# Row sums by GpSimd's queue, a fourth raw weight buffer, and later row sums for the last head, in a hybrid decoder trunk

## The chip, the cores and the metric

The kernel runs on one core of a Trainium2 chip. The metric is the device time of one execution in microseconds (us). The engines are named as the profile names them: PE (TensorE, the matmuls), PEld (its weight loads), DVE (VectorE), ACT (ScalarE), POOL (GpSimd) and SP (SyncE, which here only issues DMAs; SPq in the views).

## The reference

Two layers (DEPTH = 2) of one mixer sub-layer each, over 512 tokens (SEQ) and 16 meta tokens put ahead of them, with model width 1024, all in float32. A layer projects the normed input with one combined matrix, and mixes it in two ways at once: by causal pooling over windows of 2, 4, 8 and 16 tokens, and by latent attention with 8 heads (64 plain and 32 rotary dimensions for queries and keys, 64 for values). Both results are gated and projected back:

```python
# per layer, h = RMSNorm(x)
[u_pool | z_pool | c_q | c_kv | k_rope | z_mla | g_pool | g_mla] = h @ W_in
y_pool = W_pool_up( PoolMix(u_pool) * silu(z_pool) )
y_mla  = W_mla_up( MLA(c_q, c_kv, k_rope) * silu(z_mla) )
x = x + W_out( sigmoid(g_pool) * y_pool + sigmoid(g_mla) * y_mla )
# inside MLA, for each head, causal, over 16 + 512 positions
p = softmax(s)                 # divides by the row sum of exp(s)
o = p @ v
```

The output are the 512 tokens after both layers.

## The kernel before, in words

*Products.* Tokens stand on the free axis, 264 columns at a time (two halves of 528) in layer 0 and where meta tokens are needed, 512 at a time where they are not. Each float32 product is made of three matmuls of split operands (`mm3`, lines 211 to 213): a weight chunk is split into `whi` (ACT, L206) and `wlo` (DVE, L207), an activation into a high and a low part, `hh` and `hl` for the normed input.

*Weights.* `stream()` goes through a plan of weight products in chunks of 128 x 512 elements. `wload` gives a chunk a raw buffer (tag `raw`, 3 of them, filled by a 256 KB DMA on SP's queue, L136), and then splits it; `whi` and `wlo` have three buffers each. It is called four chunks ahead. A raw buffer is free again when the subtraction L207 has read it. The names behind `raw<-` are the matrices: `win`, then `wmu` (the attention's up projection) and so on.

*Order.* The program is recorded in one pass: `step()` records the next piece of the weight stream and adds its length to a clock (`clk`, in nanoseconds of matmul time); `after(ns, fn)` records `fn` when that clock is `ns` further on; `fill(...)` and `gap()` let the stream run between the steps of a head. `behind(ins, other)` makes an instruction wait for another one, here always the matmul that was newest when it was recorded (`newest[0]`), so that a DMA or copy isn't put far ahead of its place. `follow(ins, other)` sets an order only. Each engine, and each issuer of DMAs, then works through its instructions in order.

*A head.* `head(h, ...)` makes four blocks of scores (tile `S`), takes the causal mask and the maximum (L843), the exponential on ACT (L850, with row sums `rs`), and turns the probabilities into 32 x 32 blocks (`turn`; the 16 meta columns go by POOL into `pm`, L853). The blocks go through memory: `pdr<-attD` (L916) writes them, and `back()` reads them in four DMAs, `attE<-pdr` (L924), `BACK` = 7800 ns of matmul time later. ACT and DVE split attE into `th` and a rest (L972, L973), and `pv` multiplies it by the values (L994, L997). That product isn't yet divided by the row sums. DVE takes their reciprocals (L910), in a tile of 128 x 4. `back()` writes them to memory as one row (`rdr<-rs`, L927), `sums()` reads the row back as a broadcast onto 64 partitions (`cq<-rdr`, L934), two heads into one tile, and for each pair `gate()` multiplies the broadcast into the gate `silu(z_mla)` (POOL, L938, `u<-u,cq`). In `part2` the pair's product is multiplied by it (L1013), `LAG` = 2000 being the unit of its delay. All the writes and reads of this paragraph are on SP's queue, between the weight loads. A read of the broadcast waits on SP until the write has landed.

*Copies.* `prep(h)` puts together the keys and queries of a coming head, with copies on POOL: L817 and L819 for the keys (`kh`, `kl`), L821 for the queries (`qhl`). `ev_mu` evicts the up projection's accumulator (`mm`, one of four buffers) and stands near the end of the attention, with the eviction of `gm` (DVE L1058, ACT L1059) ahead of it.

Of the kernel before, what the change touches and what calls it, by code (L numbers as in the profile page):

```python
# [9 lines left out]
F32 = mybir.dt.float32  # L10
# [8 lines left out]
P = 128  # L19
# [8 lines left out]
H = 8  # L28
# [27 lines left out]
LAG = 2000.0  # L56
TAIL = (9000.0, 9000.0)
SPL = 240
BACK = 7800.0
LATE = 13000.0  # L60
# [21 lines left out]
def trunk(ctx, tc, xT, xrow, mrow, pos, win, wkr, wqb, wkb, wvb, wgr, wpu, wmu, wout, gains, const, yT):  # L82
    nc = tc.nc
    pe, act, dve, gp, sp = nc.tensor, nc.scalar, nc.vector, nc.gpsimd, nc.sync
# [3 lines left out]
    wp = ctx.enter_context(tc.tile_pool(name="wp", bufs=2))  # L88
# [7 lines left out]
    def nm(s):  # L96
        uid[0] += 1
        return f"{s}_{uid[0]}"

    def slot(tag, dt=F32, bufs=1, w=W):  # L100
        return sl.tile([P, w], dt, tag=tag, name=nm(tag), bufs=bufs)
# [4 lines left out]
    def att(tag):  # L106
        return sl.tile([P, NB * P], F32 if tag == "D" else F32R, tag=f"att{tag}", name=nm(f"att{tag}"), bufs=1 if tag == "D" else 2)
# [29 lines left out]
        return raw  # L137

    def rawt():
        return wp.tile([P, 512], F32, tag="raw", name=nm("raw"), bufs=3)  # L140

    early.append(slot("rinv"))
    act.dma_start(early[0][:, 0:512], win[0, MT_CKV, :, 0:512])
    first = sp.dma_start(gn, gains)
    sp.dma_start(xb[:, 0, :T], xT[:, 0, :])
    early.append(fetch(win[0, MT_CKV + 1, :, 0:512], 512, rawt(), sp))
    sp.dma_start(xb[:, 1, :T], xT[:, 1, :])
    xt = [xb[:, k] for k in range(8)]
# [16 lines left out]
    def other_loads(made):  # L165
        for k in range(2, 8):
            behind(sp.dma_start(xb[:, k, :T], xT[:, k, :]), made)
            if k in (3, 4):
                raw = rawt()
                behind(sp.dma_start(raw, win[0, MT_CKV + k - 3, :, 512:1024]), made)  # L170
                early.append(raw)
        behind(sp.dma_start(cst, const), made)
        behind(sp.dma_start(posb[:, :T], pos.partition_broadcast(P)), made)
        dve.tensor_copy(maskw[:, 512 - P:], cst[:, C_MASK:C_MASK + P])
# [18 lines left out]
    def wload(src, n, spare, home=None):  # L193
        if home is not None:
            raw = home
            behind(sp.dma_start(raw, src), marks[-4])
        else:
            raw = early.pop(0) if early else fetch(src, n, rawt(), sp)
        loads[0] += 1
        marks.append(newest[0])  # L200
        if loads[0] <= 2 or spare:
            t = wide()
            hi, lo = t[:, 0:512], t[:, 512:1024]
        else:
            hi, lo = (wp.tile([P, 512], F32R, tag=t, name=nm(t), bufs=3) for t in ("whi", "wlo"))
        act.activation(hi[:, :n], raw[:, :n], AF.Copy)  # L206
        dve.tensor_sub(lo[:, :n], raw[:, :n], hi[:, :n].bitcast(F32))  # L207
        return hi, lo
# [7 lines left out]
    newest = [None]  # L216
# [64 lines left out]
    def after(ns, fn):  # L281
        pend.append((clk[0] + ns, fn))
        pend.sort(key=lambda e: e[0])
# [28 lines left out]
    def follow(ins, other):  # L312
        tc.add_manual_dep(ins.ins, other.ins.name,
                          mybir.DependencyInfo(mybir.DependencyClass.NoSync, mybir.DependencyReason.SCHED_ONLY))

    def behind(ins, other):
        tc.add_manual_dep(ins.ins, other.ins.name,
                          mybir.DependencyInfo(mybir.DependencyClass.Sync, mybir.DependencyReason.DATA))
# [35 lines left out]
    class Layer:  # L354
# [470 lines left out]
        def head(self, h, kq, prev):  # L825
            kh, kl, qh, ql = kq
            odd = h % 2
# [3 lines left out]
            rs = sm.tile([P, 5], F32, tag="rs", name=nm("rs"), bufs=2)  # L831
# [80 lines left out]
            row = rdr[self.l][h]  # L912
# [8 lines left out]
            def back():  # L921
                got.append(att("E"))
                for b in range(4):
                    read = sp.dma_start(got[0][32 * b:32 * b + 32, :].bitcast(F32).rearrange("k (a x) -> k a x", a=4),  # L924
                                        via[:, n * b:n * b + n].rearrange("(a k) x -> k a x", a=4))
                    behind(read, newest[0])
                follow(sp.dma_start(row.rearrange("a (p i) -> p (a i)", i=4), rs[:, 0:4]), read)  # L927
                after(BACK / 3, sums)

            def sums():  # L930
                if odd == 0:
                    self.rb = slot("cq11")
                rb = self.rb
                behind(sp.dma_start(rb[64 * odd:64 * odd + 64, 0:512], row.partition_broadcast(64)), newest[0])  # L934

            def gate():
                z, rb = self.zms[h // 2][:, NM:T].rearrange("p (i q) -> p i q", i=4), self.rb
                behind(gp.tensor_mul(z, z, rb[:, 0:512].rearrange("p (q i) -> p i q", i=4)), newest[0])  # L938

            after(BACK if h + 1 < H else BACK / 3, back)  # L940
            if odd == 1:
                after(LATE if h + 1 < H else BACK, gate)
            return h, got

        def meta_turn(self, pm):
# [362 lines left out]
```

## Time and profile before

| | |
|---|---|
| time, median of 3 runs | 755.31 us (753.53 to 755.49) |
| the profiled execution | 755.48 us |
| its span | 753.7 us |
| PE busy | 748.1 us, 99% |
| DVE, ACT, POOL busy | 562.3, 395.2, 241.8 us |
| granted TensorE clock | 1.000 |
| moved by DMA | 106.55 MB, 141 GB/s in the mean |

The time is that of the whole execution, 1.78 us more than the span, which goes from the first to the last instruction of the profile. A row of the timeline reads: start, duration, engine, line, operation, out<-in with the shapes; in brackets the idle time of the engine before it, and what ended it. A row of a list of waits reads: the engine and line that waited, what it waited for, the total in us, how often, and the longest. A tile's view gives the durations of its DMA issues in ns (min, median, max), and the first and last start.

### The profile page before, as it was taken

The numbers are of one execution on the slowest core, as the hardware profiler recorded it, in microseconds if no ns is written. First come the engines' busy times: TensorE is split into PE (matmuls) and PEld (weight loads), VectorE is DVE, ScalarE is ACT, GpSimd is POOL, SyncE is SP. The second block draws the span as 40 slices with busy tenths as digits, with TensorE's granted clock in tenths as the row PEclk, the third lists the DMA queues.
The fourth block names the chain that finished last, engine by engine and source line by source line (L and its number), as shares of the span: only waits on it lengthen the run. The fifth ranks groups of instructions, "written<-read, shape, count | busy, mean of one in ns | idle before, by whom it ended". The sixth has DMA issues, their size and how long they took to land.

```text
span 753.7 us, 14317 instructions
## 1 busy us (share of the span) xinstructions
PE 748.1 (99%) x5010; PEld 681.9 (90%) x5010; DVE 562.3 (75%) x1214; ACT 395.2 (52%) x864; POOL 241.8 (32%) x294
## 2 busy tenths in 40 slices
PE   9999999999999999999999999999999999999998
PEld 9999899999999999999997898887788888887887
DVE  5588777658999987694367478678589999966942
ACT  6755656554656555543254456455445665554321
POOL 2126404704552520161130264038043526102400
PEclk9999999999999999999999999999999999999999
DMA  8633223434766576425643332233356666763462
GB/s 280 179 103 118 70 81 91 112 96 142 206 163 177 170 202 176 129 91 165 183 135 91 108 113 73 82 91 107 105 151 216 181 175 189 203 167 98 129 223 87
DMA packets 72798, 106.55 MB, mean 141 GB/s; under 512 B 14051, under 2 KB 34915, under 8 KB 72726
## 3 DMA queue, kind: packets, MB, share of 16 engines
q1 hardware_dynamic: 72582, 105.38, 47.8%
q8 instruction: 39, 0.64, 0.4%
q14 instruction: 33, 0.27, 0.1%
q10 hardware_dynamic: 144, 0.26, 0.1%
HBM read 89.76 MB, written 15.85 MB: 140 GB/s over the span
## 4 chain that ended last, share of the span: by engine, by line
PE 94%; DMA 4%; SPq 1%; DVE 1%; ACT 0%; issue 0%; ACTq 0%; DVEq 0%
PE mm L211 28%; PE mm L213 28%; PE mm L212 28%; PE S L211 2%; PE S L213 2%; PE S L212 2%; DMA raw<-wmu 1%; PE o L994 1%; DMA rdr<-rs 1%; PE o L997 1%; PE S L891 1%; PE S L538 1%; PE S L504 0%; DMA raw<-win 0%; DMA cq<-rdr 0%; DMA xb<-xT 0%
## 5 line engine op out<-in xcount | busy, mean ns | idle before, releaser
L213 PE MATMUL mm<-hh,wlo 128*128 128x264 f32 (+2 forms) x1072 | 337.0, 316 | 0.0
L212 PE MATMUL mm<-hl,whi 128*128 128x264 f32 (+2 forms) x1072 | 336.4, 315 | 0.0
L211 PE MATMUL mm<-hh,whi 128*128 128x264 f32 (+2 forms) x1072 | 336.3, 315 | 0.0
L207 DVE TENSOR_TENSOR wlo<-raw,whi 128x512 fp32r<-128x512 f32 (+2 forms) x239 | 179.6, 754 | 87.5 <-ACT whi L206 83.9
L206 ACT ACTIVATE whi<-raw 128x512 fp32r<-128x512 f32 (+2 forms) x239 | 143.0, 600 | 167.3 <-PE mm L212 133.2
L211 PEld LDWEIGHTS mm<-hh,whi 128*128 128x128 f32 x1072 | 201.4, 188 | 14.1 <-DVE vt L704 0.8
L212 PEld LDWEIGHTS mm<-hl,whi 128*128 128x128 f32 x1072 | 201.6, 188 | 13.0
L213 PEld LDWEIGHTS mm<-hh,wlo 128*128 128x128 f32 x1072 | 200.9, 188 | 12.3
L652 POOL TENSOR_TENSOR racc<-racc,tmp 128x264 f32<-128x264 f32 (+1 forms) x15 | 14.9, 993 | 117.7 <-ACT tmp L651 117.7
L1069 POOL TENSOR_TENSOR tmp<-tmp,xb 128x264 f32<-128x264 f32 (+1 forms) x24 | 27.7, 1166 | 41.8 <-DVE tmp L1067 39.7
L821 POOL CAST qhl<-q 32x528 fp32r<-32x528 f32 (+1 forms) x32 | 27.6, 876 | 40.5 <-PE S L891 39.1
L843 DVE CUSTOM_DVE_ANT_0 S<-S,maskw,nqs 128x240 f32<-128x240 f32 (+4 forms) x80 | 37.9, 493 | 1.5 <-PE S L213 1.3
L211 PE MATMUL mm<-cq,whi 128*128 128x264 f32 (+1 forms) x108 | 34.7, 321 | 0.0
L212 PE MATMUL mm<-th,whi 128*128 128x264 f32 (+1 forms) x108 | 34.6, 321 | 0.0
L213 PE MATMUL mm<-u,wlo 128*128 128x264 f32 (+1 forms) x108 | 34.5, 320 | 0.0
L212 PE MATMUL mm<-cq,whi 128*128 128x264 f32 (+1 forms) x108 | 34.5, 321 | 0.0
L213 PE MATMUL mm<-cq,wlo 128*128 128x264 f32 (+1 forms) x108 | 34.5, 321 | 0.0
L211 PE MATMUL mm<-u,whi 128*128 128x264 f32 (+1 forms) x108 | 34.5, 319 | 0.0
L938 POOL TENSOR_TENSOR u<-u,cq 128x512 f32<-128x512 f32 x8 | 12.9, 1616 | 64.6 <-DMA cq<-rdr 41.2
L853 POOL COPY pm<-cq 128x16 f32<-128x16 f32 x32 | 17.9, 559 | 44.4 <-ACT cq L850 42.3
L850 ACT ACTIVATE cq<-S,bia 128x400 f32<-128x400 f32 (+2 forms) x48 | 24.4, 512 | 13.9 <-DVE bia L904 12.8
L973 DVE TENSOR_TENSOR attE<-attE,th 128x640 fp32r<-128x640 f32 x32 | 25.6, 828 | 6.1 <-ACT th L972 6.1
(305 smaller groups left out, 1401.2 us busy)
## 6 DMA issues: line engine op xcount, KB each, us to landing
raw<-win SPq DMA_DIRECT2D x143, 256.0 KB, 3.5
pdr<-attD SPq DMA_DIRECT2D x16, 640.0 KB, 3.6
attE<-pdr SPq DMA_DIRECT2D x64, 160.0 KB, 3.6
raw<-wout SPq DMA_DIRECT2D x32, 256.0 KB, 3.0
raw<-wpu SPq DMA_DIRECT2D x16, 256.0 KB, 2.7
raw<-wmu SPq DMA_DIRECT2D x16, 256.0 KB, 2.7
raw<-wqb SPq DMA_DIRECT2D x12, 256.0 KB, 2.6
xb<-xT SPq DMA_DIRECT2D x8, 264.0 KB, 5.6
```

The costliest lines, as they stand in the source:

```text
L206: act.activation(hi[:, :n], raw[:, :n], AF.Copy)
L207: dve.tensor_sub(lo[:, :n], raw[:, :n], hi[:, :n].bitcast(F32))
L211: first = pe.matmul(out, wh, xh, start=start, stop=False)
L212: pe.matmul(out, wh, xl, start=False, stop=False)
L213: newest[0] = pe.matmul(out, wl, xh, start=False, stop=stop)
L652: self.acc_last = gp.tensor_add(self.acc[:, a:b], self.acc[:, a:b], t[:, :b - a])
L821: gp.tensor_copy(d[r0:r0 + 32, x0:T], f[gq:gq + 32, x0:T])
L843: return dve.tensor_tensor_reduce(out=sv, in0=sv, in1=mask, scale=nqs[:, i, h:h + 1], scalar=3e38, op0=ALU.add, op1=ALU.min, accum_out=bia ...
L850: act.activation(pv, sv, AF.Exp, scale=-1.0, bias=bia[:, i:i + 1], accum_out=rs[:, c:c + 1])
L853: gp.tensor_copy(pm[:, i, 16 * odd:16 * odd + 16], pt[i][:, 0:NM])
L973: dve.tensor_sub(got[:, a:b], f[:, a:b], hi[:, a:b].bitcast(F32))
L1069: gp.tensor_add(t[:, :b - a], t[:, :b - a], self.am[m][:, a:b])
```

## The change

Four things change. The pool of raw weight buffers has 4 instead of 3. The write of a head's row sums and the read of their broadcast are issued by POOL (`gp.dma_start`). The write is tied to the newest matmul, instead of standing behind the reads of attE; the read was tied so before. For the last head of a layer the write is recorded `LAG` after `back()`, the read `LAG + BACK / 3` after it, and the pair's gate at `BACK + LAG` instead of `BACK`.

```diff
     def rawt():
-        return wp.tile([P, 512], F32, tag="raw", name=nm("raw"), bufs=3)
+        return wp.tile([P, 512], F32, tag="raw", name=nm("raw"), bufs=4)
...
-                follow(sp.dma_start(row.rearrange("a (p i) -> p (a i)", i=4), rs[:, 0:4]), read)
-                after(BACK / 3, sums)
+
+                def leave():
+                    behind(gp.dma_start(row.rearrange("a (p i) -> p (a i)", i=4), rs[:, 0:4]), newest[0])
+                    after(BACK / 3, sums)
+
+                if h + 1 < H:
+                    leave()
+                else:
+                    after(LAG, lambda: behind(gp.dma_start(row.rearrange("a (p i) -> p (a i)", i=4), rs[:, 0:4]), newest[0]))
+                    after(LAG + BACK / 3, sums)
...
-                behind(sp.dma_start(rb[64 * odd:64 * odd + 64, 0:512], row.partition_broadcast(64)), newest[0])
+                behind(gp.dma_start(rb[64 * odd:64 * odd + 64, 0:512], row.partition_broadcast(64)), newest[0])
...
             if odd == 1:
-                after(LATE if h + 1 < H else BACK, gate)
+                after(LATE if h + 1 < H else BACK + LAG, gate)
```

The lines behind the change move by eight: L938 is L946 after it, L955 is L963, L959 is L967, L1013 is L1021.

SP's queue at the end of layer 1's attention, before; pdr and attE are the last head's probabilities, mdr and racc its meta columns, rdr_143 its row sums:

```order
L136 DMA raw_8798<-win 128x512
L916 DMA pdr_126<-attD_8560 128x1280
L136 DMA raw_8821<-win 128x512
L959 DMA mdr<-cq_1548_8653 128x256
L924 DMA attE_8716<-pdr_126 32x4x320 x4
L927 DMA rdr_143<-rs_8559 128x4
L136 DMA raw_8853<-win 128x512
L136 DMA raw_8872<-wmu 128x512
L934 DMA cq_1558_8707<-rdr_143 64x512
L136 DMA raw_8901<-wmu 128x512
L955 DMA racc_8817<-mdr 32x4x128 x3
L136 DMA raw_8924<-wmu 128x512
```

and the same queue after the change:

```order
L136 DMA raw_8821<-win 128x512
L916 DMA pdr_126<-attD_8560 128x1280
L136 DMA raw_8853<-win 128x512
L967 DMA mdr<-cq_1548_8653 128x256
L924 DMA attE_8716<-pdr_126 32x4x320 x4
L136 DMA raw_8872<-wmu 128x512
L136 DMA raw_8901<-wmu 128x512
L136 DMA raw_8924<-wmu 128x512
L963 DMA racc_8817<-mdr 32x4x128 x3
```

The row sums' two rows are gone, and each raw load stands one load earlier against the attention's transfers: raw_8853 is ahead of the attE reads now, and three loads of wmu are ahead of the racc reads, where two were.

POOL's instructions at head 4 of layer 0, with what the change adds marked by + (rdr_132 are the head's row sums; the copies make the keys and queries of later heads):

```order
+L929 DMA rdr_132<-rs_3428 128x4
 L853 COPY pm_3429<-cq_621_3655 128x16
+L942 DMA cq_645_3770<-rdr_132 64x512
 L821 COPY qhl_109<-q_329_1885 32x528
+L821 COPY qhl_110<-q_330_1886 32x528
 L819 COPY kh_3728<-cq_522_3030 32x528
-L821 COPY qhl_110<-q_330_1886 32x528
 L817 COPY kh_3728<-kh_3730 64x528
 L819 COPY kl_3729<-cq_523_3031 32x528
```

The write and, behind one small copy, the read of the broadcast stand directly ahead of six copies now, and POOL takes these after the read is issued.

PE's matmuls at the first scores of head 2 of layer 0 (`S_2961`; `mm_2992` is a product of the weight stream):

```order
 L211 MATMUL mm_2992<-hh_12_152,whi_2987 128x264
 L212 MATMUL mm_2992<-hl_13_153,whi_2987 128x264
+L213 MATMUL mm_2992<-hh_12_152,wlo_2988 128x264
+L211 MATMUL mm_2992<-hh_14_154,whi_2987 128x264
+L212 MATMUL mm_2992<-hl_15_155,whi_2987 128x264
+L213 MATMUL mm_2992<-hh_14_154,wlo_2988 128x264
+L211 MATMUL mm_2992<-hh_16_156,whi_2987 128x264
+L212 MATMUL mm_2992<-hl_17_157,whi_2987 128x264
+L213 MATMUL mm_2992<-hh_16_156,wlo_2988 128x264
+L211 MATMUL mm_2992<-hh_18_158,whi_2987 128x264
+L212 MATMUL mm_2992<-hl_19_159,whi_2987 128x264
 L211 MATMUL S_2961<-kh_2797,qhl_107 128x272
```

Nine matmuls of the weight stream, which stood behind these scores, stand ahead of them now. PE has the same number of instructions before and after.

## The prediction

> **What bounds the kernel now.** I read the engines' busy time first, then what TensorE (PE) waited for, then the timeline and the chain of waits around those places.
>
> ```profile
> PE   748.1 (99%) x5010; PEld 681.9 (90%) x5010; DVE 562.3 (75%) x1214; ACT 395.2 (52%) x864; POOL 241.8 (32%) x294
> ```
>
> ```profile
> PE mm L211 <- DVE cq L1058: 1.1, 1, 1.1
> PE wps L158 <- DVE na L774: 1.1, 1, 1.1
> PE S L994 <- ACT th L972: 0.2, 1, 0.2
> ```
>
> PE is busy for 748.1 of the span of 753.7 us, and the change takes no matmul away and adds none. All that it can bring lies in the remaining 5.6 us. Of the three waits that the view lists for PE itself, the second is the start of the program, before the first weights are there; the two others are stalls in the middle. Both stand at the last head of a layer. The timeline around the larger one, and the chain of waits that leads to it, read so:
>
> ```profile
> 685.93 0.39 PE L212 MATMUL mm<-kn,th 128*128 128x512 f32 x1
> 686.16 0.40 PE L213 MATMUL mm<-q,th 128*128 128x512 f32 x1
> 687.70 0.47 PE L211 MATMUL mm<-q,whi 128*128 128x512 f32 x1 [1.14 <-DVE cq L1058]
> ```
>
> ```profile
> 673.61 0.45 SPq L934
> 674.15 5.58 DMA raw<-wmu
> ...
> 684.02 0.64 ACT th L206
> ...
> 686.86 0.70 DVE cq L1058
> ```
>
> Matmuls of 512 columns start every 0.23 us (685.93 to 686.16). The one after that comes 1.54 us later, at 687.70, so the stall is 1.54 - 0.23 = **1.30 us** (by the unrounded starts, too). It waits for the eviction L1058, which frees the accumulator. DVE does that only after the splits of weight chunks, and those wait for loads that were issued late: the load at 674.15 left right after the broadcast read at 673.61, which had held SP's queue until the row sums were in memory.
>
> The smaller stall ends layer 0 in the same way:
>
> ```profile
> 302.04 0.64 ACT L206 ACTIVATE whi<-raw 128x512 fp32r<-128x512 f32 x1 [2.65 <-DMA raw<-win]
> 303.38 0.28 PE L212 MATMUL mm<-hl,whi 128*128 128x264 f32 x1
> 303.50 0.28 PE L213 MATMUL mm<-hh,wlo 128*128 128x264 f32 x1
> 303.98 0.51 PE L994 MATMUL S<-th,vt 128*128 128x512 f32 x1 [0.19 <-ACT th L972]
> ```
>
> The pace is 0.12 us here, the gap is 303.98 - 303.50 = 0.48, so the stall is **0.36 us**. ACT would have copied attE into th (L972) sooner, but stood in its order behind a weight chunk that it waited 2.65 us for.
>
> **The change part by part.** SP's queue, its own waits, the DMAs that move, and the landing of the write, from the views of their tiles:
>
> ```profile
> SPq L136 <- DVE wlo L207: 242.8, 129, 7.3
> SPq L934 <- DMA rdr<-rs: 39.9, 15, 4.1
> ```
>
> ```profile
> L927 SPq DMA_DIRECT2D rdr<-rs x16: 377/430/1749, 192.9 to 669.5; - x16
> L934 SPq DMA_DIRECT2D cq<-rdr x16: 450/450/451, 198.0 to 673.6; - x16
> ```
>
> ```profile
> DMA to landing us min/median/max: 3.3/3.6/4.1
> ```
>
> *Removed from SP.* 16 writes of 0.43 us and 16 reads of 0.45 us leave its queue, 14 us of issue, and with them 39.9 us in 15 waits for a write to land, 2.7 us each. None of this is on PE's path except where a weight load or an attE read behind it was late and something waited: the two stalls. Elsewhere the weight loads wait 242.8 us for a free raw buffer, that is, they are early anyway. So 14 heads give nothing, and the last heads give 1.30 + 0.36.
>
> *The fourth raw buffer* lets each load go one chunk earlier. Whether that reaches the 687 stall is read from SP's queue, from the splits that free the buffers, and from the ACT instruction ahead of the copy at 684.02:
>
> ```profile
> 669.51 1.75 SPq L927 DMA_DIRECT2D rdr<-rs  x1
> 671.83 0.38 SPq L136 DMA_DIRECT2D raw<-wmu  x1
> 674.15 0.54 SPq L136 DMA_DIRECT2D raw<-wmu  x1
> ```
>
> ```profile
> 667.59 0.68 DVE L207 TENSOR_TENSOR wlo<-raw,whi 128x512 fp32r<-128x512 f32 x1
> 668.79 0.69 DVE L207 TENSOR_TENSOR wlo<-raw,whi 128x512 fp32r<-128x512 f32 x1
> ```
>
> ```profile
> 681.83 0.63 ACT L1059 ACTIVATE cq<-cq 128x512 f32<-128x512 f32 x1 [0.92 <-DVE cq L1058]
> ```
>
> With four buffers the first two loads of wmu follow the splits that end at 668.3 and 669.5, where they were issued at 671.83 and 674.15: 3.5 and 4.7 us earlier, and the next follow in the same way. ACT's copy at 684.02 then no longer waits. In ACT's order the work before it ends at 682.5 (L1059, 0.63 from 681.83), so about 1.5 us are won; DVE's split behind it and what follows there move as much, and L1058 ends near 686.0, before 686.16 + 0.23 = 686.39, where PE wants the accumulator. The whole 1.30 goes, with 0.4 us to spare. At 303.98 the reads of attE were issued by 294.8 and land 2.7 to 5.0 us later, as their tile's view has it:
>
> ```profile
> 293.39 1.39 SPq L924 DMA_DIRECT2D attE<-pdr  x3
> ```
>
> ```profile
> DMA to landing us min/median/max: 2.7/3.6/5.0
> ```
>
> So th could be made from 299.8 on, and the 0.36 goes too.
>
> *Added on GpSimd (POOL).* 32 DMAs, and a new wait: the broadcast waits for its write's landing on POOL, and the pm copies, the key and query copies of the head after next and the gate stand behind it. The trace has no DMA issued by POOL. Bounds for write issue, landing and broadcast issue together (call it x): from SP's rows 0.43 + about 3.6 + 0.45 = 4.5 us; with SP's slowest issue for each and its longest wait, 1.75 + 4.1 + 1.75 = 7.6. I take 5 to 6, nearer to the lower end, since only one of the 32 issues was slow. What x may be is read where copies stand closest behind a broadcast, at heads 0 and 4 of layer 0:
>
> ```profile
> 189.88 0.28 PE L212 MATMUL mm<-hl,whi 128*128 128x264 f32 x1
> 191.87 0.63 POOL L819 CAST kl<-cq 32x528 fp32r<-32x528 f32 x1 [0.42 <-PE S L891]
> 195.17 0.62 POOL L819 CAST kh<-cq 32x528 fp32r<-32x528 f32 x1
> 202.25 0.29 PE L211 MATMUL S<-kh,qhl 96*128 96x272 f32 x1
> ```
>
> ```profile
> 248.11 0.28 PE L212 MATMUL mm<-hl,whi 128*128 128x264 f32 x1
> 251.76 0.62 POOL L821 CAST qhl<-q 32x528 fp32r<-32x528 f32 x1
> 255.98 0.96 POOL L817 CAST kl<-kl 64x528 fp32r<-64x528 f32 x1
> 260.82 0.47 PE L211 MATMUL S<-kh,qhl 96*128 96x272 f32 x2
> ```
>
> The write is tied to the matmul that was newest when it was recorded, the first row of each group. The second and third row of a group are the first and the last of the copies. Head 0: the copies take 191.87 to 195.79, 3.9 us; the scores that need them start at 202.25, and 1.1 later in the new order (nine matmuls of 0.12 ahead of them), so x may be 203.35 - 189.88 - 3.9 = 9.5 us. Head 4: 251.76 to 256.94, 5.2 us, so x may be 260.82 - 248.11 - 5.2 = 7.5 us. With 5 to 6, both hide it: nothing. At 7.6 it is 0.1.
>
> *The last head's sums later.* The write stood at 669.51, behind the four attE reads and their slow issue; on POOL it waits for neither, and the gate stands next behind the broadcast. At x of 5 to 6 the gate is no later than before, where the broadcast read itself went at 673.61. I count nothing; by how much it could be early doesn't matter, since the pair's product is only wanted after the eviction at 686.86.
>
> *Order.* The planner shifts heads' scores by about 1 us of other matmuls and the last head's pv is 0.9 us earlier, while th for it (an L972 after attE) isn't: 0 to 0.3 us of a new short stall; I take 0.1.
>
> **The sum**, on the profiled execution (755.48, the span and 1.78 us around it): 755.48 - 1.30 - 0.36 + 0.1 = 753.9 us. The median of the runs, 755.31, is 0.17 below the profiled one. The forecast is **753.9**, 0.19% below the median. About 0.3%, 2.27 us, is what a measurement of this kernel can tell from no change: under 753.04 counts as faster, over 757.58 as slower. Its own range is 753.4 (one more short wait gone) to 754.8 (half of the 687 stall kept).
>
> **The rivals.**
>
> *POOL becomes the bound (slower).* Work on POOL is drawn out at times, and the issue of a DMA there may be too. The same small copy, 128 x 16, takes
>
> ```profile
> 245.44 0.20 POOL L853 COPY pm<-pa 128x16 f32<-128x16 f32 x1
> 249.44 2.25 POOL L853 COPY pm<-cq 128x16 f32<-128x16 f32 x1 [1.33 <-ACT cq L850]
> ```
>
> 0.20 or 2.25 us. If the issue of a write of 128 partitions takes two such stretches (4.5) and the broadcast one (2.25), x is 4.5 + 4.1 + 2.25 = 10.85: 1.35 over the margin at head 0, 3.35 at head 4, together 4.7, and 753.9 + 4.7 = **758.6**. It decides from x = (9.5 + 7.5 + 3.7) / 2 = 10.35 on, where the loss passes 757.58. For it: the in-order wait, and DVE at 75%. Against: POOL is busy 32% only, and in other heads the copies stand farther off.
>
> The Trainium skill ("SBUF — State Buffer", "SBUF: two separate sides") states a rule of this kind: a GpSimd DMA can't write its descriptors while DVE holds the port they share, and one of 620 ns alone took about 3100 ns beside DVE copies. By its figure x would be an estimated 3.1 + 3.6 + 3.1 = 9.8, 0.3 + 2.3 us over, some 756.5. The trace's stretched copies agree in direction only; the chance of this is a part of POOL's, below.
>
> *The stall only moves (no change).* The loads come earlier, but ACT works in order, and its weight copies mostly wait not for data but for PE to free a buffer:
>
> ```profile
> ACT whi L206 <- PE mm L212: 136.1, 105, 2.8
> ```
>
> If the wait for PE replaces the wait for data at 684.02, the fourth buffer doesn't do what it could, and only 0.36 goes: 755.48 - 0.36 = **755.1**. Against it: the 687 chain names a raw load, not PE.
>
> *More than the stalls goes (faster).* Weight loads of PE wait too:
>
> ```profile
> PEld mm L211 <- DVE vt L704: 0.8, 2, 0.4
> ```
>
> If earlier loads take that 0.8 as well, it is 755.48 - 1.66 - 0.8 = **753.0**, just faster. Against: those waits end with a DVE step that is no weight split.
>
> **How the numbers follow.** Forecast 0.37, POOL 0.33, stall moved 0.10, more gone 0.20. A tenth of POOL's chance is a loss that stays below 757.58 (x of 7.5 to 10.35). Within 0.3% are that 0.03, the forecast and the moved stall: 0.50. Faster: 0.20. Slower: the rest of POOL's, 0.30. The range goes from 752.7, a little past the third rival, to 759.0, a little past POOL's price, since longer stretches or more heads would go on from there (about 0.1).
>
> **What would show it.** Right: no PE wait for L1058 near 686, none for L972 near 303; the raw loads of wmu issued by about 668 to 673; POOL waits for rdr of 3 to 4 us that nobody waits for. Wrong: PE or ACT waits for key copies (L817, L819, L821) ahead of scores, POOL DMA issues of over 2 us, a landing of over 6, or a stall at the same accumulator with ACT named for PE.

## The result, and the profile after

The changed kernel takes **760.20 us** (median of 6 runs, 759.29 to 760.75) against 754.71 before (6 runs, 753.53 to 755.49): 1.0072 of it, with a 95% interval of 1.0061 to 1.0082. The forecast was 753.9 in a range of 752.7 to 759.0. It is slower, and by more than the range held. The profiled execution has a span of 758.8 us, 5.1 more than before.

The engines' busy time and what PE waited for, after:

```profile
PE 749.2 (99%) x5010; PEld 681.9 (90%) x5010; DVE 560.3 (74%) x1214; ACT 395.3 (52%) x864; POOL 260.3 (34%) x326
```

```profile
PE S L1002 <- ACT th L980: 2.4, 1, 2.4
PE mm L211 <- ACT whi L206: 1.3, 2, 0.8
PE o L1002 <- ACT th L980: 1.3, 2, 1.1
PE wps L158 <- DVE na L774: 1.1, 1, 1.1
PE S L211 <- ACT hh L377: 0.2, 1, 0.2
```

The two stalls of before are gone (no wait for L1058, which is L1066 now, and none at layer 0's last head), and others have come: 5.2 us in four rows that end with ACT, none with POOL. L980 is L972 of before: ACT's copy of attE, that is, PE waits for probabilities read back from memory. The largest stall, in the timeline of PE and ACT:

```profile
678.46 0.40 PE L212 MATMUL mm<-hl,whi 128*128 128x512 f32 x1
681.25 0.51 PE L1002 MATMUL S<-th,vt 128*128 128x512 f32 x1 [2.40 <-ACT th L980]
```

```profile
679.84 1.36 ACT L980 ACTIVATE th<-attE 128x640 fp32r<-128x640 f32 x2 [5.07 <-DMA attE<-pdr]
```

The start-to-start gap is 2.79 us where the pace is 0.23, so 2.56 us are lost here. ACT stood idle in front of it for 5.07 us. The chain of waits says what came so late:

```profile
670.46 0.37 SPq L924
670.88 0.49 SPq L924
671.42 0.42 SPq L924
671.89 7.87 DMA attE<-pdr
679.84 1.37 ACT th L980 x2
681.25 0.51 PE S L1002
```

The last of the four attE reads was issued at 671.89 and was on its way for 7.87 us. That isn't one bad transfer. The landings of all 64 attE reads, from the view of their tile (min, median, max; before it was 2.7, 3.6 and 5.0):

```profile
DMA to landing us min/median/max: 2.6/4.8/7.9
```

The reads are of the same size, on the same queue and issued by the same engine as before, and take 1.2 us longer in the median. SP's own waits show where a head's next step is held up by such delays:

```profile
SPq L924 <- DMA pdr<-attD: 34.2, 14, 4.9
SPq L963 <- DMA mdr<-cq: 30.0, 6, 6.3
```

The waits of the racc reads for the meta columns' write (L963, L955 before) came to 30.0 us in 6 waits, and the next head's pdr write stands behind them. What GpSimd's queue was forecast to do wrong, it doesn't. Its DMAs, from the view of tile rdr, and its wait for the write's landing:

```profile
L942 POOL DMA_DIRECT2D cq<-rdr x16: 530/530/556, 195.5 to 675.1; - x16
L929 POOL DMA_DIRECT2D rdr<-rs x14: 567/572/710, 189.8 to 655.7; - x14
...
DMA to landing us min/median/max: 1.9/3.7/7.3
```

```profile
POOL cq L942 <- DMA rdr<-rs: 14.9, 6, 4.1
```

An issue takes 0.53 to 0.71 us on POOL, and it waited only 6 times for a write to land. Nobody waits for a key copy.

### The profile page after: what moved, and what is told of

Same layout as the page of the kernel before. It is cut to its first block, busy times and chain, and to the rows that moved or that the text cites. A ratio compares the mean times of both kernels' runs of the same rounds, so it can differ in the third digit from the quotient of the medians.

```text
span 758.8 us, 14338 instructions
## 1 busy us (share of the span) xinstructions
PE 749.2 (99%) x5010; PEld 681.9 (90%) x5010; DVE 560.3 (74%) x1214; ACT 395.3 (52%) x864; POOL 260.3 (34%) x326
## 3 DMA queue, kind: packets, MB, share of 16 engines
q0 software_dynamic: 1280, 2.13, 1.1%
## 4 chain that ended last, share of the span: by engine, by line
PE 89%; DMA 5%; DVE 3%; ACT 1%; SPq 1%; issue 0%; ACTq 0%; DVEq 0%
PE mm L211 27%; PE mm L213 27%; PE mm L212 27%; DMA attE<-pdr 2%; PE S L211 2%; PE S L212 2%; PE S L213 2%; DMA pdr<-attD 1%; DMA mdr<-cq 1%; PE o L1002 1%; DVE wlo L207 1%; PE o L1005 1%; PE S L538 1%; ACT th L980 1%; PE S L891 0%; DVE attD L856 0%
## 5 line engine op out<-in xcount | busy, mean ns | idle before, releaser
L207 DVE TENSOR_TENSOR wlo<-raw,whi 128x512 fp32r<-128x512 f32 (+2 forms) x239 | 176.8, 742 | 82.6 <-ACT whi L206 76.2
L819 POOL CAST kh<-cq 32x528 fp32r<-32x528 f32 x16 | 15.9, 992 | 44.6 <-ACT cq L309 43.9
L980 ACT ACTIVATE th<-attE 128x640 fp32r<-128x640 f32 x32 | 21.8, 729 | 14.4 <-DMA attE<-pdr 9.7
```

Of the source, the lines that this page charges most:

```text
L819: gp.tensor_copy(d[r0:r0 + 32, :], f[g0:g0 + 32, :])
L980: behind(act.activation(hi[:, a:b], f[:, a:b], AF.Copy), newest[0])
```

## The experiments

Each kernel is compared with runs of the kernel before on the same chip; their medians are 754.1 to 754.5 us.

### Which of the three edits

Three theories. A: the fourth raw buffer lets weight loads crowd in ahead of the attention's transfers. B: DMAs of GpSimd are slow and slow the others. C: the later sums of the last head.

`e1_buf4`, the buffer alone, on the kernel before:

```diff
-        return wp.tile([P, 512], F32, tag="raw", name=nm("raw"), bufs=3)
+        return wp.tile([P, 512], F32, tag="raw", name=nm("raw"), bufs=4)
```

> Before with one line changed: four raw buffers instead of three; SP still issues the row sums. Theory A (the fourth buffer lets weight loads stand and move ahead of the attention's transfers, so attE lands late): 758 to 760 us, with a wait of PE for L972 of 1 us or more at a layer's last heads. Theory B (DMAs issued by GpSimd are slow and slow the others): 753 to 755 us. Theory C (the later sums of the last head): 753 to 755 us.

754.07 us, 0.9999 of before (0.9990 to 1.0008). `e2_gp`, both DMAs on GpSimd, nothing else:

```diff
-                follow(sp.dma_start(row.rearrange("a (p i) -> p (a i)", i=4), rs[:, 0:4]), read)
-                after(BACK / 3, sums)
+                def leave():
+                    behind(gp.dma_start(row.rearrange("a (p i) -> p (a i)", i=4), rs[:, 0:4]), newest[0])
+                    after(BACK / 3, sums)
+                leave()
...
-                behind(sp.dma_start(rb[64 * odd:64 * odd + 64, 0:512], row.partition_broadcast(64)), newest[0])
+                behind(gp.dma_start(rb[64 * odd:64 * odd + 64, 0:512], row.partition_broadcast(64)), newest[0])
```

> Before with the row sums' write and broadcast issued by GpSimd alone: three raw buffers, the last head's sums as early as the others'. Theory A: 753.5 to 755 us, landings of attE back at about 3.6 us. Theory B: 758 to 760 us, landings of attE at 4.8 us as after the whole change. Theory C: 753.5 to 755 us.

760.46 us, 1.0073 (1.0047 to 1.0099). `e3_gp_late`, the whole change but the buffer (`bufs=4` back to `bufs=3`):

> The changed kernel with three raw buffers instead of four. Theory A: 753.5 to 755 us, the 2.6 us wait of PE for the last head's attE gone. Theory B and theory C: 759 to 760 us, that wait still there.

760.80 us, 1.0076 (1.0053 to 1.0100). `e5_gp_buf4`, the whole change but the later sums (`leave()` for all heads, the gate at `BACK`):

> The changed kernel with the last head's sums no later than the other heads'. Theory A and theory B: 759 to 761 us. Theory C: 753.5 to 755 us.

759.76 us, 1.0081 (1.0050 to 1.0112). So the buffer and the later sums do nothing that can be measured, and the step that moves the two DMAs to GpSimd, and ties the write to the newest matmul, is the whole loss: A and C fall. Landings of attE in `e1_buf4`, and in `e2_gp`:

```profile
DMA to landing us min/median/max: 2.6/3.5/4.7
```

```profile
DMA to landing us min/median/max: 3.1/4.9/6.6
```

### Which of the two DMAs

Three theories again. R: SP's queue, without its wait for the row sums, lets loads crowd around the write mdr, and the racc reads that wait for it hold the next pdr write. S: transfers of GpSimd's queue slow the others. P: the other order of PE's matmuls.

`f1_gp_read`, the kernel before with the broadcast alone on GpSimd:

```diff
-                behind(sp.dma_start(rb[64 * odd:64 * odd + 64, 0:512], row.partition_broadcast(64)), newest[0])
+                behind(gp.dma_start(rb[64 * odd:64 * odd + 64, 0:512], row.partition_broadcast(64)), newest[0])
```

> Before with only the broadcast read issued by GpSimd; the row sums' write stays on SP behind the attE reads. Theory R (without the broadcast's wait on SP, weight loads crowd around the meta columns' write mdr; racc reads wait for it on SP and hold the next head's pdr write): 758 to 760 us, SP's waits of racc for mdr near 30 us in all. Theory S (transfers of GpSimd's queue themselves slow the others): 758 to 760 us as well, with landings of attE at 4.8 us. Theory P (the other order of PE's matmuls costs it): 754 to 756 us, since this kernel's order of matmuls differs from before's in a third of the rows that it differs in after the change.

754.27 us, 1.0002 (0.9992 to 1.0011), landings of attE at

```profile
DMA to landing us min/median/max: 2.5/3.4/5.4
```

`f2_gp_write`, the write alone on GpSimd, tied to the newest matmul, the broadcast on SP (the first part of `e2_gp`'s diff):

> Before with only the row sums' write issued by GpSimd, tied to the newest matmul; the broadcast stays on SP and waits there. Theory R: 753.5 to 755.5 us, racc's waits for mdr near 9 us in all. Theory S: 753.5 to 756 us, since the write has 2 KB of the 130. Theory P: 754 to 756 us.

756.46 us, 1.0026 (1.0015 to 1.0036), landings of attE at

```profile
DMA to landing us min/median/max: 2.7/4.8/6.1
```

This was what no theory had expected. The broadcast, 64 times the write's bytes, may go to GpSimd for nothing, and frees SP of its waits for nothing. The write of 2 KB makes the reads of attE late. R and S fall as causes of the late landings. The time doesn't follow from the landings alone, though: they are as late here as in `e2_gp`, and the loss is 2.2 us instead of 6.4.

`f3_gp_racc_later`, `e2_gp` with the racc reads of the first three pairs recorded just behind the next head's pdr write:

```diff
...
-            after(LATE, back)
+            if h + 1 < H:
+                self.read_meta = back
+            else:
+                after(LATE, back)
...
             if odd == 1:
+                if h + 1 < H:
+                    self.read_meta()
                 op, mt = self.op[:, NM:T], self.mt
```

> The kernel with both DMAs on GpSimd (three raw buffers, sums of the last head as the others'), and the racc reads of the first three pairs recorded just behind the next head's pdr write, so that they can't hold it on SP. Theory R: 754 to 757 us, pdr writes back within 0.5 us of the last turn. Theory S: 759 to 761 us, since the slow landings stay. Theory P: 758 to 761 us.

760.57 us, 1.0077 (1.0058 to 1.0096). SP no longer waits for mdr, and PE waits for racc itself instead:

```profile
PE mm L1018 <- DMA racc<-mdr: 3.6, 3, 1.6
PE S L1001 <- ACT th L979: 1.2, 1, 1.2
```

Taking the wait off SP only hands it on; the transfers are late.

### The write: its engine, its place, its memory

What differs for the write is the engine, and its place: before, `follow(..., read)` puts it behind the four attE reads; after, it is tied to the matmul that is newest there and is issued ahead of them, by 0.1 to 5.3 us in the changed kernel (1.3 in the median). Theory W: a write of GpSimd holds up SP's queue. Theory O: the place ahead of the reads, and the order that comes with it.

`g1_sp_write_tied`, `e2_gp` with the write on SP again, but tied as there, so that it differs from `f1_gp_read` only in `behind(..., newest[0])` for `follow(..., read)`:

```diff
-                    behind(gp.dma_start(row.rearrange("a (p i) -> p (a i)", i=4), rs[:, 0:4]), newest[0])
+                    behind(sp.dma_start(row.rearrange("a (p i) -> p (a i)", i=4), rs[:, 0:4]), newest[0])
```

> As the kernel with both DMAs on GpSimd, but the row sums' write is issued by SP, tied to the newest matmul as there; the broadcast stays on GpSimd. Theory W (a write that GpSimd issues while the attE reads are in flight holds the packets of SP's queue up, and attE lands 1.5 us later): 753.5 to 755.5 us, landings of attE near 3.5 us. Theory O (the write's place ahead of the attE reads, and the order of instructions that comes with it): 757 to 761 us, landings of attE near 4.8 us.

760.25 us, 1.0076 (1.0054 to 1.0097), with no write on GpSimd at all. `g3_act_write`, the same with `act.dma_start`:

> As the kernel with both DMAs on GpSimd, but the write is issued by ACT's queue, tied as there; the broadcast stays on GpSimd. Theory W: 753.5 to 756 us (ACT gives some 0.4 us of issue a head, with slack), landings of attE near 3.5 us. Theory O: 757 to 761 us, landings of attE near 4.8 us.

761.63 us, 1.0094 (1.0076 to 1.0112). Theory W falls. The landings of attE in these two:

```profile
DMA to landing us min/median/max: 3.1/4.4/7.0
```

```profile
DMA to landing us min/median/max: 2.7/4.3/7.6
```

`g2_gp_write_later` was to put GpSimd's write behind the reads by `after(2000, leave)`:

> Both DMAs on GpSimd, but the write is recorded 2000 ns of matmul time later than the attE reads, for all heads, and the broadcast 1000 later than before, so that the write's packets come when most of attE has landed. Theory W: 753.5 to 756 us, landings of attE at 3.4 to 4.2 us. Theory O: no sharp forecast, 754 to 760 us, since this order is again another. If landings of attE stay near 4.8 us, theory W falls.

760.42 us, 1.0073 (1.0053 to 1.0092), landings at 4.0. It settles little, since half of the writes came ahead of the reads all the same: the reads wait for pdr, the write doesn't.

`g4_extra_gp_write` leaves the kernel before as it is, nearly all of its order of instructions included, and adds a write that nobody needs, at the place in question:

```diff
+    spare = [[dp.tile([1, SEQ], F32, name=f"spare{l}{h}") for h in range(H)] for l in range(DEPTH)]
...
+                behind(gp.dma_start(spare[self.l][h].rearrange("a (p i) -> p (a i)", i=4), rs[:, 0:4]), newest[0])
                 follow(sp.dma_start(row.rearrange("a (p i) -> p (a i)", i=4), rs[:, 0:4]), read)
```

> Before, with its row sums on SP as they were, and one more write of the same 2 KB for each head, issued by GpSimd behind the newest matmul at the attE reads, into memory that nobody reads. The order of everything else is nearly that of before. Theory W: landings of attE at 4.5 to 5 us, 754.5 to 757 us. Theory O: landings near 3.6 us, 753.5 to 755 us.

761.38 us, 1.0085 (1.0064 to 1.0107), landings of attE at 4.7: 16 writes of 2 KB cost 7 us. Theory W had the landing right and the time too low; with `g1_sp_write_tied` it is the place, not the issuer. From here theory M: a small write to main memory ahead of the reads holds them up; against it theory G: any further DMA of GpSimd costs it.

`h3_extra_gp_sbuf` is `g4_extra_gp_write` with the target on the chip, and the same order of instructions:

```diff
-    spare = [[dp.tile([1, SEQ], F32, name=f"spare{l}{h}") for h in range(H)] for l in range(DEPTH)]
+    spare = [[cp.tile([P, 4], F32, name=f"spare{l}{h}") for h in range(H)] for l in range(DEPTH)]
...
-                behind(gp.dma_start(spare[self.l][h].rearrange("a (p i) -> p (a i)", i=4), rs[:, 0:4]), newest[0])
+                behind(gp.dma_start(spare[self.l][h], rs[:, 0:4]), newest[0])
```

> The extra 2 KB write of GpSimd stands at the attE reads, in the same order of instructions, but goes into a tile of the on-chip memory instead of the device's main memory. Theory M, if a write to main memory is what counts: 753.5 to 755.5 us, landings of attE near 3.6 us. If any small DMA there does it: 759 to 762 us, landings near 4.7 us. Theory G: 759 to 762 us.

755.16 us, 1.0019 (1.0010 to 1.0029). Landings of attE in `g4_extra_gp_write` and in `h3_extra_gp_sbuf`:

```profile
DMA to landing us min/median/max: 2.5/4.7/7.0
```

```profile
DMA to landing us min/median/max: 2.7/3.6/5.2
```

In this pair PE and SP work through the same rows in the same order; it differs in where 2 KB go, and in 6.2 us. How the reads are held can be counted in the trace's packet records, here the 512 packets of 1280 bytes of the third head of layer 1, started in each 0.5 us, counted from the first read's issue (the column 0.5 goes from 0.5 to 1.0; none starts earlier):

```
us from the issue       0.5  1.0  1.5  2.0  2.5  3.0  3.5  4.0  4.5  5.0
before                    7   64  126   80   73  101   49   11    1    0
write to main memory      4   46   22    8   42  113  150   89   32    6
write on the chip         7   61  126   97   82   93   46    0    0    0
```

Thirteen of the 16 packets of the write to main memory start just ahead of the first read's issue, and those of the write on the chip at 0.7 us. With the former the reads begin at the same time, almost stop for 1.5 us, and go on at full rate.

The two writes of this head don't come at the same time: GpSimd issued one 1.27 us ahead of the reads and the other 0.43 us. That isn't the cause. In six heads the two kernels agree in this distance within 0.1 us, and in each of them the last packet of the reads ends 0.8 to 1.7 us later with the write to main memory. The distance counts within `g4_extra_gp_write`: in the 12 heads with the write 1.1 to 3.4 us ahead, the last packet ends 5.2 to 7.5 us after the first read's issue; in three of the other four, with 3.6 to 5.4 us, at 4.3 to 4.5.

The 6.2 us aren't waiting alone. Between the two profiled executions PE's listed waits differ by 2.5 us (4.6 and 2.1), and its busy time, for the same matmuls, by 3.4 (751.0 and 747.6). Half of the latter is the clock that PE was granted behind its stall at the last head of layer 1 in `g4_extra_gp_write`:

```profile
680.73 0.50 PE L996 MATMUL S<-th,vt 128*128 128x512 f32 x1 [1.76 <-ACT th L974]
682.21 0.63 PE L211 MATMUL mm<-hh,whi 128*128 128x512 f32 x1
682.63 0.63 PE L212 MATMUL mm<-hl,whi 128*128 128x512 f32 x1
```

```profile
681.30:684.50 3.20, 3.20 (x9) 0.50 0.79 222
684.80:688.00 3.20, 3.20 (x18) 1.00 0.47 131
```

A row of the second view is a stretch, its length, PE's busy time and matmuls, the granted clock, the DMA engines' busy share and GB/s. The clock was half for 3.4 us, matmuls of 512 columns started every 0.42 us instead of 0.23, and 1.7 us were lost. Eight of the 18 profiled executions here have such a stretch, next to stalls of 1.0 to 5.0 us; the changed kernel's has none, with a stall of 2.40. So late data can cost more than the time that PE waits for them.

`h2_extra_gp_later` records the extra write to main memory 5000 ns later than the reads:

```diff
-                behind(gp.dma_start(spare[self.l][h].rearrange("a (p i) -> p (a i)", i=4), rs[:, 0:4]), newest[0])
+                after(5000, lambda: behind(gp.dma_start(spare[self.l][h].rearrange("a (p i) -> p (a i)", i=4), rs[:, 0:4]), newest[0]))
```

> Before with its row sums on SP as they were, and the extra 2 KB write issued by GpSimd as in the kernel with one, but recorded 5000 ns of matmul time after the attE reads instead of at them. Theory M (a write to memory whose packets come just ahead of the attE reads, whoever issues it, holds these reads up by about 1.4 us): 753.5 to 755.5 us, landings of attE near 3.6 us. Theory G (one more DMA of GpSimd a head costs it, wherever it stands): 759 to 762 us.

759.67 us, 1.0067 (1.0045 to 1.0089). Both theories missed. Landings of attE are back at 3.5, as M has it, but the time isn't. The write of the head before fell on attE's reads mainly at the last head of each layer. PE's waits in this kernel:

```profile
PE S L211 <- ACT cq L851: 2.0, 1, 2.0
PE S L996 <- ACT th L974: 1.3, 1, 1.3
```

The second is the last head's. Behind the first the clock was half for 3.4 us too; of the four runs the three with a mean clock of 0.998 took 759.3 to 760.3 us, and the one with 1.000 took 756.47. For the first, the chain of waits goes back to a pdr write that was issued at 219.08 behind racc reads, 2.6 us later than before's third. So a write off the attE reads can still make PE wait elsewhere; that it does so by holding other transfers is only argued.

### Without the write in that place, and without its memory

`h4_gp_read_buf4`, what is left of the change if the write stays behind the reads on SP (`f1_gp_read` with four raw buffers):

> What is left of the change when the write stays on SP behind the attE reads: GpSimd issues the broadcast, and there are four raw buffers. Theory M: 753 to 754.5 us, no stall at a layer's last heads; it may be the fastest of all by a few tenths. Theory G: 753 to 755 us, since the broadcast alone cost nothing.

754.25 us, 1.0004 (0.9994 to 1.0013). No wait of PE is left in its profile but those at the start of the program, and it is no faster than before. No version here is.

`j1_gp_write_sbuf` is `e2_gp` with the write's target on the chip. The broadcast reads rows that are filled with ones once, at the start, so the division by the row sums is left out, and the broadcast no longer waits for the write:

```diff
+            gp.dma_start(rdr[l][h].rearrange("a (p i) -> p (a i)", p=4), ones[0:4, :])
...
-                    behind(gp.dma_start(row.rearrange("a (p i) -> p (a i)", i=4), rs[:, 0:4]), newest[0])
+                    behind(gp.dma_start(spare[self.l][h], rs[:, 0:4]), newest[0])
```

> The kernel with both DMAs on GpSimd (three raw buffers, sums of the last head as the others'), but each head's 2 KB write goes into an on-chip tile; the rows in main memory are filled once with ones at the start, and the broadcast reads these, so the division by the row sums is left out. The order of instructions is nearly the same. Theory M (a small write to main memory holds the reads up that are on their way): 754 to 756 us, landings of attE at 3.5 to 3.9 us, 4.5 us or more under that kernel. Theory O (the other order, or SP without its waits, costs it): 759 to 761 us, landings of attE near 4.9 us.

757.42 us, 1.0041 (1.0023 to 1.0058), landings of attE at 3.7 instead of 4.9. It lies between: the loss is 3.0 us, where `e2_gp` has 6.4, so about half goes with the memory write. The rest doesn't: PE still waits 1.3 us for the last head's attE.

`i2_gp_write_behind` keeps the write in memory and on GpSimd, and makes it wait for the last attE read's landing (`behind(..., read)` for `behind(..., newest[0])`):

> Both DMAs on GpSimd, but the write waits on POOL until the last of the head's four attE reads has landed. Theory M: landings of attE at 3.4 to 3.9 us, since no write stands ahead of them, and 754 to 757 us: the write still comes among weight loads, and POOL waits some 4 us more a head. The forecast's rival (POOL's in-order wait pushes the key copies): 757 to 762 us, with PE or ACT waiting for L817, L819 or L821. Theory O: landings of attE stay near 4.9 us.

762.97 us, 1.0120 (1.0084 to 1.0157). Landings of attE are at 3.4, again as M has it, and the time is the worst of all. The sums come late: the first broadcast starts at 212.6 and the last at 686.6, where before had 198.0 and 673.6,

```profile
L938 POOL DMA_DIRECT2D cq<-rdr x16: 520/526/535, 212.6 to 686.6; - x16
```

and PE waits in many small places, none of them for a key copy. That the late sums cause these waits isn't shown.

## Why the prediction was wrong, point by point

**The step that failed** is the place of the write. The prediction saw that "on POOL it waits for neither" the attE reads nor their slow issue, and counted that at nothing: the write was weighed by its issue, its landing and who waits for it, as is right for the engines. What it does to the transfers behind it was not asked: it makes the attE reads land at 4.8 instead of 3.6 us, and PE waits 3.7 us for them (the two rows of L980). `g4_extra_gp_write` and `h3_extra_gp_sbuf` show that a write does this: 6.2 us between a target in main memory and one on the chip, in the same order. `f1_gp_read` and `g1_sp_write_tied` show that it is the place and not GpSimd: 754.27 with the write behind the reads, 760.25 with it tied, both times on SP and with the broadcast on GpSimd.

**Removed from SP.** That the 39.9 us of waits and 14 us of issue were worth nothing outside the last heads was right: `f1_gp_read` takes 16 of the 32 DMAs and all those waits off SP, and measures 1.0002.

**The fourth buffer, and the term of 1.66 us.** What `e1_buf4` shows fits the mechanism. Its waits of PE and its first loads of wmu are these:

```profile
PE wps L158 <- DVE na L774: 1.1, 1, 1.1
PE S L211 <- ACT hh L377: 0.5, 2, 0.3
```

```profile
668.82 2.19 SPq L136 DMA_DIRECT2D raw<-wmu  x2
```

The loads go from 668.82 on (before 671.83 and 674.15; the prediction had 668.3), and no wait for L1058 or L972 is left. The term was mis-sized: it measured nothing, 754.07 against 754.09 for before. The profiled execution of before, at 755.48, was among the slowest of its runs, whose median over 14 others was 754.09. The two stalls were a feature of that execution, as far as the median goes; whether faster executions of before have them isn't known, as only this one was profiled. The larger one isn't peculiar to it: `h3_extra_gp_sbuf`, with three buffers and a profiled execution near its median, has a wait of 0.7 us for the same eviction. In the changed kernel the loads weren't even early: the first wmu load stands behind attE reads that are themselves late:

```profile
670.46 1.87 SPq L924 DMA_DIRECT2D attE<-pdr  x4
672.43 4.10 SPq L136 DMA_DIRECT2D raw<-wmu  x3
```

**Added on GpSimd.** That the margins hide it was right, though x came out a little longer. The term x, from the write's issue to the broadcast's, was forecast at 5 to 6 us against margins of 9.5 and 7.5. At head 0 it was 195.51 + 0.54 - 189.83 = 6.2:

```profile
189.83 0.71 POOL L929 DMA_DIRECT2D rdr<-rs  x1
...
195.51 0.54 POOL L942 DMA_DIRECT2D cq<-rdr  x1 [4.09 <-DMA rdr<-rs]
...
198.04 0.62 POOL L819 CAST kh<-cq 32x528 fp32r<-32x528 f32 x1
```

These copies are done at 198.66, and the scores start at 203.33.

**The slower rival** had the sign and, at 758.6, nearly the time, but by luck, since the cause was another: nobody waited for a copy. The rule beside it, from the Trainium skill ("SBUF — State Buffer", "SBUF: two separate sides"), had GpSimd's DMAs starved while DVE holds a port they share. No run here shows that: the 16 issues of the broadcast took 0.53 to 0.56 us, with DVE busy 74% of the span. What the skill gives for such a DMA ("DMA: Bandwidth & Descriptors", "Anatomy of one DMA — SWDGE (gpsimd) path"), about 2.0 us and the bytes at 436 GB/s, would be an estimated 2.0 us for the write and 2.3 for the broadcast. In the changed kernel the medians are 3.6 and 4.4. The 4.4 isn't GpSimd's own time. In `f1_gp_read`, without the write ahead of the reads, the broadcast takes

```profile
cq<-rdr POOLq DMA_DIRECT2D x16, 128.0 KB, 3.5
```

and on SP, before,

```profile
cq<-rdr SPq DMA_DIRECT2D x16, 128.0 KB, 3.1
```

and 5.1 on SP in `f2_gp_write`, with the write ahead. The measurement decides, here against the estimate.

**Order.** The last head's pv was to wait 0 to 0.3 us; it waits 2.4, for the reason above.

**What stays open.** How a write of 2 KB holds up reads of another buffer isn't seen from here, only that it does. And not all of the loss is that: about half of it stays in `j1_gp_write_sbuf`, which has the changed order of instructions and no such write, and `h2_extra_gp_later` and `i2_gp_write_behind` are slow with good landings of attE. Nor is it known why the two DMAs cost 6.4 us together, where the write alone costs 2.2 and the broadcast alone nothing; two of the four runs of `e2_gp` have a mean clock of 0.998, and none of the eight of `f2_gp_write`, but the other two of `e2_gp`, at 1.000, still took 757.89 and 759.84 us.

## What to carry to other kernels

Before a small DMA is moved, ask which transfers will be behind it in time, not only who waits for it: a write to main memory just ahead of reads that the critical engine needs can cost more than the waits that the move saves. When one edit moves a transfer to another engine and also changes what it is ordered behind, test the two apart; here the engine was free, and the write's place cost up to 0.8%. And a term read from one profiled execution is only worth what the median has of it: compare that execution with the runs first.

## What the runs showed of the hardware

A write of 2 KB to main memory from 128 partitions, issued by GpSimd 1.1 to 5.4 us ahead of reads of 640 KB, holds these up: their landings go from 3.6 to 4.7 us in the median. Where the row sums' write itself stands ahead they are at 4.8 with GpSimd, 4.4 with SP and 4.3 with ACT as the issuer. The same transfer into on-chip memory leaves them at 3.6. Behind the reads on one queue it cost nothing that was seen. Next to stalls of PE of 1.0 to 5.0 us, though not to each, the granted clock was half for 3.4 us, and for 6.8 us once. GpSimd issues a DMA in 0.52 to 0.72 us. Where the row sums' write is behind the reads, a broadcast of 128 KB lands after 3.4 to 3.5 us by GpSimd and 3.0 to 3.5 by SP; where it is tied to the matmul, mostly ahead of them, after 4.4 in the changed kernel, by GpSimd, and 5.1 in `f2_gp_write`, by SP.
